# Attention with unscaled exponentials turned, inverse row sums passed through DRAM, and a pair's result divided well behind its softmax

## The chip, the cores and the metric

The kernel runs on one core of a Trainium2 chip as one program. Its time is the device time of one execution in microseconds. Before the change it is 2454.31 us, the median of three runs (2453.69 to 2454.6).

The profile takes one more execution apart, engine by engine. PE is TensorE's matmul side and PEld its weight loads. DVE is VectorE, ACT is ScalarE, POOL is GpSimd, and SP is SyncE, which here does little but issue loads. A name such as L962 is a line of the kernel, numbered as in the version before unless "of after" stands with it. A row of the trace names a tile that is written and the tiles read (`t<-t,rs`), and its shape as partitions x elements.

## What is computed

Two layers of a streaming encoder over 512 tokens of width 1024. A layer is a feed-forward part, a mixer and another feed-forward part. The mixer has three branches: A is attention with a learned bias by distance, B multi-scale pooling, C attention with forget gates. The change concerns A and C alone, with 8 heads of width 64 each.

```python
# branch A (chunked) and branch C (causal), per head
p = softmax(logits + bias, axis=-1)        # over the keys
out = einsum('bhnqk,bnkhd->bnqhd', p, v)
...
branch = einsum('bsnw,nwd->bsnd', stack([ya, yb, yc], axis=2), w_branch)
gates = sigmoid(g_lin.reshape(B, S, 3, D_MODEL))
merged = sum_n(gates * branch)
return merged @ w_out
```

The softmax divides each row of exponentials by its sum. The product with v is linear in the row, so that the division may stand before it or behind it.

## The kernel before

**Numbers in two parts.** Almost every product is made of three matmuls: an operand is kept as a high part (fp32r) and the rest that the rounding leaves (lo). `triple` (L117 to L122) issues hi x hi, hi x lo and lo x hi. `split_to` (L377 to L379) makes such a pair: ACT casts the high part (L378), and DVE, or another engine where one is given, subtracts it from the source (L379).

**The order of work.** The program counts its matmul work in `pe[0]`; one unit is a matmul of 128x512. `later(delay, fn, group)` puts a piece of work on a list, due at `pe[0] + delay`; `poll()` runs what is due, `poll(group="a")` all that belongs to branch A, and `poll(True)` all there is. So a delay such as LAG_T = 24 says how many units of other matmuls are issued between a piece of work and the next that depends on it. A scheduler then decides the order on each engine and which buffer a tile gets; tiles of one tag take turns in a fixed number of buffers (17 of "b", 3 of "t2", 2 of "t1", 2 of "strip", 1 of "ssum"; 4 each of "mm" and "acc" in PSUM).

**Attention** (L940) runs once for A and once for C in each layer: 4 times, 32 heads, 128 query tiles, 16 pairs of heads. For head h and query tile i (128 queries, (i+1)*128 keys):

- `logits`: PE makes the scores with two matmuls (L951, L952; L953 and L954 of after). DVE subtracts them from the bias strip and takes the row's extreme in one instruction (L955). ACT takes the exponential and sums the row (L959). DVE inverts the sum (L961), and the exponentials are multiplied by it in place, on POOL for i < 3 and on DVE for i = 3 (L962).
- `turn`, LAG_T = 24 units later: PE transposes the row blocks (L974), ACT casts the high part out of PSUM (L978), DVE makes the low part (L979). They go to tiles "pta" and "ptb".
- `weigh`, LAG_V = 14 units after every second turn: PE multiplies by v (L996, L997), 256 queries at a time. Both parts of v stand beside each other, so that a head's result comes out in two halves of partitions; ACT copies one (L1000) and DVE adds the other (L1001). `split_to` splits the sum, 64x256, with ACT for the high part and POOL for the low part.

A tile of `ys` holds the two heads of a pair on its 128 partitions, high and low parts of all 512 queries.

Between the query tiles a "filler" issues other matmuls: during A's attention the projections of q, k and v for C and its forget gates; during C's attention the merge of branch A (`merge_units`), which reads `ys`. Ahead of the merge's first product `poll(group="a")` forces everything of A that is still on the list.

POOL's other work in these stretches: a fill of A's bias strips behind their load (L926), masks of C's strips (L937), and in the mixer's later part additions of the merge. SP issues the loads of weights and strips. The copy of x to DRAM is issued from POOL (L1119).

Of the kernel before, what the change touches and what calls it, by code (L numbers as in the profile page):

```python
# [15 lines left out]
F32 = mybir.dt.float32  # L16
F32R = mybir.dt.float32r
I32 = mybir.dt.int32
AF = mybir.ActivationFunctionType
ALU = mybir.AluOpType  # L20
AX = mybir.AxisListType

P = 128
T = 512
# [6 lines left out]
HD = 64  # L31
NT = T // P
# [8 lines left out]
def encoder_kernel(tc, xT, c, w_ada, b_ada, gains, w_gate, w_up, w_down, w_qkv, w_f, w_ubg,  # L41
                   qk_gain, rel, fbias, w_pool, pool_scale, w_branch, w_out, inv_cnt, w_first, out):
    nc = tc.nc
    pools = []

    def open_pool(**kw):
        p = tc.tile_pool(**kw)
        pools.append(p)
        return p.__enter__()
# [4 lines left out]
    dr = open_pool(name="dr", bufs=1, space=bass.MemoryType.DRAM)  # L54
# [3 lines left out]
    NB, NRAW = 17, 2  # L58

    def nm(s):  # L60
        uid[0] += 1
        return f"{s}_{uid[0]}"

    def st(shape, dt, tag, bufs):
        return sb.tile(shape, dt, tag=tag, bufs=bufs, name=nm(tag))
# [4 lines left out]
    def mmt(shape=(P, T)):  # L70
        return ps.tile(list(shape), F32, tag="mm", bufs=4, name=nm("mm"))

    def blk(tag, dt=F32R):
        bufs = {"xv": 4, "v2": 4, "b": NB}[tag]
        return st([P, 2, T], dt, tag, bufs)

    def t1(cols=T):
        return st([P, cols], F32, "t1", 2)

    def t2(cols=T):  # L80
        return st([P, cols], F32, "t2", 3)
# [16 lines left out]
    def later(delay, fn, group=None):  # L98
        t = Task(pe[0] + delay, fn, group)
        tasks.append(t)  # L100
        return t

    def poll(everything=False, group=None):
        if polling[0]:
            return
        polling[0] = True
        while True:
            ready = [t for t in tasks if t.fn is None or everything or t.due <= pe[0]
                     or (group is not None and t.group == group)]
            if not ready:  # L110
                break
            t = min(ready, key=lambda z: z.due)
            tasks.remove(t)
            t.run()
        polling[0] = False
# [56 lines left out]

    x_dram = dr.tile([4, P, 2 * T], F32, name="x_dram")
    fv_dram = [dr.tile([H, FVLEN], F32, name=f"fv_dram{l}") for l in range(L)]

    last = {}

# [199 lines left out]
    def split_to(hi, lo, src, lo_eng=nc.vector):  # L377
        nc.scalar.copy(hi, src)  # L378
        lo_eng.tensor_tensor(lo, src, hi.bitcast(F32), op=ALU.subtract)  # L379
# [502 lines left out]
    def finish_turns(upto=3):  # L882

        for todo in turns:
            while len(todo) >= 4 - upto:
                todo.pop(0)()
# [53 lines left out]
    def attention(qs, ks, vs, strip, ys, filler, budget, group):  # L940


        open_pt = {}

        def logits(h, i, strips):
            p, off = divmod(h, 2)
            (q, ql), k = qs[p], ks[p]
            odd = h % 2
            n = (i + 1) * P
            s = mmt()  # L950
            mm(s[:, :n], q[:, odd, i * P:(i + 1) * P], k[:, odd, :n], start=True, stop=False)  # L951
            mm(s[:, :n], ql[:, odd, i * P:(i + 1) * P], k[:, odd, :n], start=False, stop=True)  # L952
            lg = t1(T)[:, :n]  # L953
            mx = st([P, 1], F32, "mx", 4)  # L954
            nc.vector.tensor_tensor_reduce(out=lg, in0=s[:, :n], in1=strips[i], scale=-1.0, scalar=BIG,  # L955
                                           op0=ALU.add, op1=ALU.min, accum_out=mx)
            pr = t2(T)[:, :n]
            sm = st([P, 1], F32, "sm", 4)
            nc.scalar.activation(pr, lg, AF.Exp, bias=mx, scale=-1.0, accum_out=sm)  # L959
            rs = st([P, 1], F32, "rs", 4)  # L960
            nc.vector.reciprocal(rs, sm)  # L961
            (nc.vector if i == NT - 1 else nc.gpsimd).tensor_scalar(pr, pr, rs, None, op0=ALU.mult)  # L962
            pe[0] += 0.5 * (i + 1.5)
            later(LAG_T, lambda: turn(h, i, pr), group)

        def turn(h, i, pr):
            half, c = divmod(i, 2)
            nj = 2 * half + 2
            if c == 0:
                open_pt[h] = st([P, 2, nj, 256], F32R, "ptb" if half else "pta", 2 if half else 1)  # L970
            pt = open_pt[h]
            tp = mmt()
            for j in range(i + 1):
                nc.tensor.transpose(tp[:, j * P:(j + 1) * P], pr[:, j * P:(j + 1) * P], ident)  # L974
            tv = tp[:, :(i + 1) * P].rearrange("p (j q) -> p j q", q=P)
            dh = pt[:, 0, :i + 1, c * P:(c + 1) * P]
            dl = pt[:, 1, :i + 1, c * P:(c + 1) * P]
            nc.scalar.copy(dh, tv)  # L978
            nc.vector.tensor_tensor(dl, tv, dh.bitcast(F32), op=ALU.subtract)  # L979
            pe[0] += 0.55 * (i + 1)  # L980
            if c == 1:
                later(LAG_V, lambda: weigh(h, half, pt), group)

        def weigh(h, half, pt):
            p, off = divmod(h, 2)
            rows = slice(off * HD, off * HD + HD)
            other = slice(HD - off * HD, 2 * HD - off * HD)
            if off == 0 and half == 0:
                ys.append(blk("b"))
            y = ys[p]  # L990
            o = mmt((P, HALF))
            nj = 2 * half + 2
            for j in range(nj):
                q0 = P if j == nj - 1 else 0
                v2 = vs[j][:, h, :, :].rearrange("p a d -> p (a d)")
                mm(o[:, q0:], v2, pt[:, 0, j, q0:], start=(j == 0), stop=False)  # L996
                mm(o[:, q0:], v2, pt[:, 1, j, q0:], start=False, stop=(j == nj - 1))  # L997
            cols = slice(half * HALF, (half + 1) * HALF)
            yl = t1(T)[:, :HALF]
            nc.scalar.copy(yl[rows, :], o[other, :])  # L1000
            nc.vector.tensor_tensor(yl[rows, :], o[rows, :], yl[rows, :], op=ALU.add)  # L1001
            split_to(y[rows, 0, cols], y[rows, 1, cols], yl[rows, :], nc.gpsimd)
            pe[0] += 1.0 * nj

        for h in range(H):
            strips = strip(h)
            if group == "c":
                finish_turns(h // 2)
            for i in range(NT):
                logits(h, i, strips)  # L1010
                if i == NT - 1:
                    heads[0] = h + 1
                poll()
                goal = pe[0] + budget
                while filler is not None and pe[0] < goal:
                    if next(filler, "end") == "end":
                        filler = None
                poll()
        if filler is not None:
            for _ in filler:  # L1020
                pass

    LAG_T, LAG_V = 24, 14


    def pool_front(l, g):
# [77 lines left out]
    class Mixer:  # L1104
# [10 lines left out]
        def run(self, nxt):  # L1115
# [19 lines left out]

            lo_share[0] = LO_SHARE
            attention(qa, ka, va, lambda h: strip_a(l, h), ya, fill_a(), FILL_A, "a")
            heads[0] = H

# [23 lines left out]
            def fill_c():  # L1163
                yield from merge_units(l, 0, ya, put_a)

            attention(qc, kc, vc, lambda h: strip_c(l, h), yc, fill_c(), FILL_C, "c")
            finish_turns()
            turns.clear()
# [102 lines left out]
```

## Time and profile before

| | |
|---|---|
| runs, median (lowest to highest) | 2454.31 us (2453.69 to 2454.6) |
| profiled execution | 2450.88 us, with a span of 2448.9 us |
| attention stretches | 490 to 700 us and 1695 to 1910 us of the span |

The span begins with the first and ends with the last instruction of the profile. The first view of a profile gives the busy time of each engine; one of the later ones the groups of instructions, each with its line, engine, operation, shape, count, busy us, mean ns, and the idle time of the engine just ahead of them. In the bracket of a row in order of time stands the idle time ahead of that instruction and what ended it. Matmuls overlap: a row's length is longer than the distance of two starts.

### The profile page before, as it was taken

The page shows a single profiled execution, that of the slowest core. Times are in us where ns is not written, and L with a number is a line of the kernel's source. Part 1 is how long each engine was busy: PE and PEld are TensorE (multiplying, and loading weights), DVE is VectorE, ACT ScalarE, POOL GpSimd, SP SyncE. Part 2 cuts the span into 40 slices and gives each one's busy share as a digit, 9 for nine tenths or more (in the row PEclk, how much of TensorE's full clock was granted, in tenths as well). Part 3 has the DMA queues.
Part 4 walks back from the last instruction along what each step waited for, and adds up shares of the span by engine and source line. Part 5 has one row for each costly group of instructions (what it writes and reads, how often), then busy time and mean ns, then how long its engine had stood idle before and what let it go on. Part 6 is the DMA issues. An engine that isn't in the chain of part 4 may idle for free. (4 is left out here: it accounts for less than half of the span.)

```text
span 2448.9 us, 34028 instructions
## 1 busy us (share of the span) xinstructions
PE 2396.8 (98%) x12966; PEld 2051.8 (84%) x12966; DVE 1600.5 (65%) x2859; ACT 1110.3 (45%) x1888; POOL 377.3 (15%) x439
## 2 busy tenths in 40 slices
PE   7999999999999999999999999999999999999999
PEld 5798888777888898988898888878777888988888
DVE  8978766677643378787678656477765434765463
ACT  5333345677642353333453334366765333533341
POOL 3000002144532110000000000123354322000000
PEclk9999999999999999999999999999999999999999
DMA  7756543222323426565327423223133234233232
GB/s 284 251 170 209 198 147 113 78 82 88 116 91 103 142 75 240 174 206 198 129 85 243 138 86 121 103 90 96 61 109 99 95 111 139 87 104 112 67 114 78
DMA packets 116279, 320.23 MB, mean 131 GB/s; under 512 B 11122, under 2 KB 13298, under 8 KB 116116
## 3 DMA queue, kind: packets, MB, share of 16 engines
q1 hardware_dynamic: 114962, 313.86, 38.3%
q0 software_dynamic: 1152, 4.19, 0.4%
q8 instruction: 102, 1.67, 0.3%
q14 instruction: 61, 0.50, 0.1%
q10 hardware_dynamic: 2, 0.00, 0.0%
HBM read 311.64 MB, written 6.38 MB: 130 GB/s over the span
## 5 line engine op out<-in xcount | busy, mean ns | idle before, releaser
L271 ACT CAST whi<-raw 128x1024 fp32r<-128x1024 f32 (+1 forms) x325 | 338.2, 1044 | 595.1 <-PE mm L120 289.2
L273 DVE TENSOR_TENSOR wlo<-raw,whi 128x1024 fp32r<-128x1024 f32 x317 | 392.2, 1240 | 197.4 <-ACT whi L271 194.2
L121 PE MATMUL mm<-hhi,wlo 128*128 128x512 f32 x744 | 289.8, 390 | 0.7 <-DVE wlo L273 0.4
L119 PE MATMUL mm<-hhi,whi 128*128 128x512 f32 x744 | 290.2, 390 | 0.0
L120 PE MATMUL mm<-hlo,whi 128*128 128x512 f32 x744 | 290.0, 390 | 0.0
L119 PE MATMUL acc<-b,whi 128*128 128x512 f32 (+1 forms) x704 | 264.1, 376 | 1.7 <-ACT b L378 1.7
L121 PE MATMUL acc<-b,wlo 128*128 128x512 f32 (+1 forms) x704 | 262.1, 374 | 3.5 <-DVE wlo L273 3.5
L120 PE MATMUL acc<-b,whi 128*128 128x512 f32 (+1 forms) x704 | 262.4, 373 | 0.0
L197 DVE CUSTOM_DVE_ANT_0 v<-v,b,badac 128x1024 f32<-128x1024 f32 x144 | 188.3, 1316 | 60.9 <-DMA v<-in_w_ada_dram 60.7
L119 PE MATMUL acc<-hhi,whi 128*128 128x512 f32 x480 | 190.7, 399 | 1.7 <-ACT hhi L738 1.7
L121 PE MATMUL acc<-hhi,wlo 128*128 128x512 f32 x480 | 188.9, 394 | 0.0
L120 PE MATMUL acc<-hlo,whi 128*128 128x512 f32 x480 | 188.5, 393 | 0.2 <-DVE hlo L741 0.2
L121 PEld LDWEIGHTS mm<-hhi,wlo 128*128 128x128 f32 x744 | 139.7, 188 | 30.9 <-DVE wlo L273 1.6
L119 PEld LDWEIGHTS mm<-hhi,whi 128*128 128x128 f32 x744 | 140.0, 188 | 27.9
L120 PEld LDWEIGHTS mm<-hlo,whi 128*128 128x128 f32 x744 | 139.7, 188 | 27.4
L121 PEld LDWEIGHTS acc<-b,wlo 128*128 128x128 f32 x704 | 133.8, 190 | 27.2 <-DVE wlo L273 4.6
L119 PEld LDWEIGHTS acc<-b,whi 128*128 128x128 f32 x704 | 133.3, 190 | 23.8 <-ACT b L378 2.6
L120 PEld LDWEIGHTS acc<-b,whi 128*128 128x128 f32 x704 | 133.3, 189 | 23.2 <-DVE b L379 0.9
L119 PE MATMUL acc<-whi,hhi 128*128 128x512 f32 x336 | 137.7, 411 | 4.4 <-ACT t L828 3.7
L120 PE MATMUL mm<-b,whi 128*128 128x512 f32 (+1 forms) x384 | 135.8, 354 | 0.0
L119 PE MATMUL mm<-b,whi 128*128 128x512 f32 (+1 forms) x384 | 135.8, 354 | 0.0
L121 PE MATMUL mm<-b,wlo 128*128 128x512 f32 (+1 forms) x384 | 135.6, 354 | 0.0
(300 smaller groups left out, 5598.3 us busy)
## 6 DMA issues: line engine op xcount, KB each, us to landing
v<-in_w_ada_dram SPq DMA_DIRECT2D x144, 512.0 KB, 4.4
raw<-in_w_down_dram SPq DMA_DIRECT2D x88, 512.0 KB, 3.5
raw<-in_w_up_dram SPq DMA_DIRECT2D x82, 512.0 KB, 3.4
b<-in_w_gate_dram SPq DMA_DIRECT2D x76, 512.0 KB, 5.3
raw<-in_w_ubg_dram SPq DMA_DIRECT2D x56, 512.0 KB, 3.3
raw<-in_w_qkv_dram SPq DMA_DIRECT2D x42, 512.0 KB, 3.7
raw<-in_w_branch_dram SPq DMA_DIRECT2D x24, 512.0 KB, 3.6
raw<-in_w_out_dram SPq DMA_DIRECT2D x16, 512.0 KB, 3.3
```

What stands on the lines that cost most here:

```text
L119: mm(o, lh, rh, start=start, stop=False, skip_group_check=onto)
L120: mm(o, lh, rl, start=False, stop=False, skip_group_check=onto)
L121: mm(o, ll, rh, start=False, stop=stop, skip_group_check=onto)
L197: dot = nc.vector.tensor_tensor_reduce(out=raw, in0=raw, in1=silc[0], scale=1.0, scalar=badac[:, l, j, d:d + 1], op0=ALU.mult, op1=ALU.add ...
L271: nc.scalar.copy(hi, raw)
L273: lo_eng.tensor_tensor(lo, raw, hi.bitcast(F32), op=ALU.subtract)
```

## The change

The reciprocals' place and the division's place are moved behind the product with v:

- The exponential's row sums of a head go to one tile [128, 4], a column for each query tile. After the fourth tile one reciprocal inverts all four columns (L965 of after). Nothing scales the exponentials; `turn` transposes them as they are.
- The inverses have queries on partitions; the result of `weigh` has queries along the row. So a DMA issued from POOL writes the [128, 4] tile to a row of DRAM in the order of the queries (L966 of after), 512 numbers of 4 bytes.
- LAG_R = 50 units later `spread` issues a second DMA from POOL: it reads the row and writes it to the 64 partitions of this head (L1011 of after), in the second half of a tile "b" named `rows_of[p]`. `weigh`'s add writes its sum straight to the first half.
- LAG_N = 36 units behind the odd head's spread, `norm_rows` takes a new tile "b", multiplies the pair's sums by the spread inverses on DVE (L1020 of after, 128x512), and splits the product with ACT and DVE (L379 and L380 of after, 128x512).

```diff
+    inv_dram = {(g, p): dr.tile([2, T], F32, name=f"inv_dram_{g}{p}") for g in "ac" for p in range(4)}
...
+        sums, rows_of = {}, {}
...
             pr = t2(T)[:, :n]
-            sm = st([P, 1], F32, "sm", 4)
-            nc.scalar.activation(pr, lg, AF.Exp, bias=mx, scale=-1.0, accum_out=sm)
-            rs = st([P, 1], F32, "rs", 4)
-            nc.vector.reciprocal(rs, sm)
-            (nc.vector if i == NT - 1 else nc.gpsimd).tensor_scalar(pr, pr, rs, None, op0=ALU.mult)
+            if i == 0:
+                sums[h] = st([P, NT], F32, "sm", 3)
+            nc.scalar.activation(pr, lg, AF.Exp, bias=mx, scale=-1.0, accum_out=sums[h][:, i:i + 1])
+            if i == NT - 1:
+                rs = st([P, NT], F32, "rs", 3)
+                nc.vector.reciprocal(rs, sums[h])
+                nc.gpsimd.dma_start(inv_dram[group, p][odd].rearrange("(i q) -> q i", q=P), rs)
+                later(LAG_R, lambda: spread(h), group)
...
             if off == 0 and half == 0:
-                ys.append(blk("b"))
-            y = ys[p]
+                rows_of[p] = st([P, 2, T], F32, "b", NB)
+            y = rows_of[p][:, 0, :]
...
             nc.scalar.copy(yl[rows, :], o[other, :])
-            nc.vector.tensor_tensor(yl[rows, :], o[rows, :], yl[rows, :], op=ALU.add)
-            split_to(y[rows, 0, cols], y[rows, 1, cols], yl[rows, :], nc.gpsimd)
+            nc.vector.tensor_tensor(y[rows, cols], o[rows, :], yl[rows, :], op=ALU.add)
             pe[0] += 1.0 * nj
+
+        def spread(h):
+            p, off = divmod(h, 2)
+            nc.gpsimd.dma_start(rows_of[p][off * HD:(off + 1) * HD, 1, :],
+                                inv_dram[group, p][off:off + 1, :].broadcast_to([HD, T]))
+            if off:
+                later(LAG_N, lambda: norm_rows(p), group)
+
+        def norm_rows(p):
+            y = blk("b")
+            ys.append(y)
+            full = rows_of[p][:, 0, :]
+            nc.vector.tensor_tensor(full, full, rows_of[p][:, 1, :], op=ALU.mult)
+            split_to(y[:, 0, :], y[:, 1, :], full)
...
-    LAG_T, LAG_V = 24, 14
+    LAG_T, LAG_V, LAG_R, LAG_N = 24, 14, 50, 36
```

The three places below show how instructions stand on an engine, in the order of its queue; there is no time in them. A row has the line, the operation, the tiles (their numbers differ between the versions) and the shape.

POOL in the attention of C, early in the first layer's: t is a tile of exponentials, rs an inverse sum, strip and ssum the bias strips, b a pair's result.

```order
L962 TENSOR_SCALAR t_1113_5638<-t_1113_5638,rs_5641 128x256
L962 TENSOR_SCALAR t_1120_5666<-t_1120_5666,rs_5669 128x384
L937 TENSOR_TENSOR strip_5898<-strip_5898,cmask 128x128 x3
L379 TENSOR_TENSOR b_5589<-t_1128_5695,b_5589 64x256
L937 TENSOR_TENSOR ssum_5743<-ssum_5743,cmask 128x128
L962 TENSOR_SCALAR t_1146_5755<-t_1146_5755,rs_5758 128x128
L379 TENSOR_TENSOR b_5589<-t_1150_5769,b_5589 64x256
L962 TENSOR_SCALAR t_1161_5800<-t_1161_5800,rs_5803 128x256
```

The same stretch of after:

```order
L938 TENSOR_TENSOR strip_5760<-strip_5760,cmask 128x128 x3
L966 DMA inv_dram_c_127<-rs_5594 128x4x1
L938 TENSOR_TENSOR ssum_5620<-ssum_5620,cmask 128x128
L1011 DMA b_5477<-inv_dram_c_127 64x512
L938 TENSOR_TENSOR strip_5902<-strip_5902,cmask 128x128 x3
L966 DMA inv_dram_c_128<-rs_5738 128x4x1
L938 TENSOR_TENSOR ssum_5762<-ssum_5762,cmask 128x128
L1011 DMA b_5780<-inv_dram_c_128 64x512
```

POOL has no scaling and no subtraction of results left there; the masks of the next head's strips now alternate with the two DMAs of a head.

DVE in the attention of C, from the end of one head's logits into the next head's: mm is a PSUM tile, pta and ptb the turned exponentials, mx the row's extreme.

```order
L961 RECIPROCAL rs_5956<-sm_5954 128x1
L979 TENSOR_TENSOR ptb_5891<-mm_5962,ptb_5891 128x4x128
L955 ISA t_1210_5978,mx_5979<-mm_5975,strip_5898 128x384
L955 ISA mx_5979 128x1
L979 TENSOR_TENSOR pta_5987<-mm_5988,pta_5987 128x128
L961 RECIPROCAL rs_5984<-sm_5982 128x1
L1001 TENSOR_TENSOR t_1218_6007<-mm_5998,t_1218_6007 64x256
L955 ISA t_1221_6023,mx_6024<-mm_6020,ssum_5900 128x512
```

The same place of after:

```order
L984 TENSOR_TENSOR ptb_5895<-mm_5961,ptb_5895 128x4x128
L957 ISA t_1185_5977,mx_5978<-mm_5974,strip_5902 128x384
L957 ISA mx_5978 128x1
L984 TENSOR_TENSOR pta_5982<-mm_5983,pta_5982 128x128
L1006 TENSOR_TENSOR b_5780<-mm_5993,t_1191_6002 64x256
L1020 TENSOR_TENSOR b_5780<-b_5780 128x512
L984 TENSOR_TENSOR pta_5982<-mm_6008,pta_5982 128x2x128
L957 ISA t_1194_6017,mx_6018<-mm_6014,ssum_5904 128x512
```

The reciprocals between are gone. The product L1020 stands directly behind the add of the odd head's last weighing, ahead of the next low part L984 and the next L957.

PE at the hand-over of A's last pair to the merge: b_5311 (before) and b_5539 (after) are the result of pair 3, whi and wlo weights of the merge, hhi and hlo the layer's input, acc the merge's sums.

```order
L951 MATMUL mm_5632<-b_5107,b_4550 128x256
L952 MATMUL mm_5632<-b_5107,b_4551 128x256
L119 MATMUL acc_5674<-b_5311,whi_5402 128x512
L120 MATMUL acc_5674<-b_5311,whi_5402 128x512
L121 MATMUL acc_5674<-b_5311,wlo_5403 128x512
```

The same place of after:

```order
L119 MATMUL acc_5662<-hhi,whi_5658 128x512
L120 MATMUL acc_5662<-hlo,whi_5658 128x512
L121 MATMUL acc_5662<-hhi,wlo_5659 128x512
L119 MATMUL acc_5553<-b_5539,whi_5299 128x512
L119 MATMUL acc_5604<-b_5539,whi_5299 128x512
L979 MATMUL mm_5612<-ident,t_1067_5549 128x128
L120 MATMUL acc_5553<-b_5539,whi_5299 128x512
```

Before, scores of a head of C stand directly ahead of the first matmul that reads the pair; in after, matmuls of a gate (hhi with whi) are placed ahead of it.

## The prediction, made before the changed kernel ran

> **What bounds the kernel now.** The page's first lines come first: who is busy, and for how long.
>
> ```profile
> span 2448.9 us, 34028 instructions
> PE 2396.8 (98%) x12966; PEld 2051.8 (84%) x12966; DVE 1600.5 (65%) x2859; ACT 1110.3 (45%) x1888; POOL 377.3 (15%) x439
> ```
>
> PE (TensorE's matmuls) is busy 98% of the span, and the change takes away no matmul and adds none. It can only win idle time of PE. POOL's 377.3 us are no limit as such; POOL matters where PE waits for it. So the second view is busy time by stretch (length, then busy us of PE, PEld, DVE, ACT, POOL with their counts), for the first layer's two attentions, for the second layer's, and for a stretch of FFN.
>
> ```profile
> 490.00:700.00 210.00, 198.19 (x1037) 159.37 (x1036) 144.55 (x375) 138.22 (x313) 98.59 (x131) 0.99 0.30 95
> 1695.00:1910.00 215.00, 201.84 (x1055) 161.14 (x1054) 147.50 (x378) 140.45 (x316) 100.42 (x133) 1.00 0.30 91
> 1100.00:1310.00 210.00, 209.18 (x1256) 186.83 (x1255) 149.97 (x262) 90.26 (x145) 9.32 (x9) 1.00 0.43 145
> ```
>
> PE stands idle for 210 - 198.19 = 11.8 us and 215 - 201.84 = 13.2 us in the attentions, 25.0 us together, and for 0.8 us in the FFN stretch. These 25 us, 1.0% of the span, are all that can be won. The third view says who ends that idle time: PE's waits (matmul line and releaser, total us, times, longest). Lines from L940 to L1001 are attention's.
>
> ```profile
> PE mm L974 <- POOL t L962: 6.8, 15, 0.7
> PE mm L951 <- DVE t L1001: 4.6, 6, 1.1
> PE mm L951 <- DVE ptb L979: 3.0, 2, 1.5
> PE mm L951 <- DVE b L859: 1.8, 2, 0.9
> PE mm L951 <- DVE mx L955: 1.8, 4, 0.7
> PE mm L974 <- DVE ptb L979: 1.7, 4, 0.5
> PE mm L974 <- DVE rs L961: 1.0, 2, 0.5
> ```
>
> The first row is the wait that the change is about: the transposes L974 wait for POOL's scaling of the exponentials. With the last row (reciprocal) that is 7.8 us in 17 waits. The other five make 12.9 us in 18 waits: logits L951 or transposes behind DVE work that came late.
>
> One such wait in order of time (start, length; the bracket is the drawn idle time):
>
> ```profile
> 513.77 0.39 PE L120 MATMUL acc<-wlo,hhi 128*128 128x512 f32 x1
> 514.00 0.40 PE L121 MATMUL acc<-whi,hlo 128*128 128x512 f32 x1
> 514.08 0.93 POOL L962 TENSOR_SCALAR t<-t,rs 128x256 f32<-128x256 f32 x1 [5.50 <-DVE rs L961]
> 515.06 0.33 PE L974 MATMUL mm<-ident,t 128*128 128x128 f32 x1 [0.66 <-POOL t L962]
> ```
>
> Matmuls follow each other every 514.00 - 513.77 = 0.23 us (my unit below), though each is drawn 0.40 long. The transpose could have started at 514.23 and started at 515.06: 0.83 us lost, 0.66 drawn. A drawn wait hides about 0.17 us more.
>
> **The change part by part.** Two layers have 4 attentions, 32 heads, 128 query tiles and 16 pairs of heads. Rows of groups: line, engine, shape and count, then busy us, mean ns, idle before.
>
> ```profile
> L961 DVE RECIPROCAL rs<-sm 128x1 f32<-128x1 f32 x128 | 20.2, 159 | 37.7 <-ACT t L959 37.6
> L962 DVE TENSOR_SCALAR t<-t,rs 128x512 f32<-128x512 f32 x32 | 16.6, 520 | 1.2
> L962 POOL TENSOR_SCALAR t<-t,rs 128x384 f32<-128x384 f32 x32 | 39.9, 1248 | 37.2 <-DVE rs L961 26.8 <-PE mm L974 5.7 <-PE acc L121 2.4
> L962 POOL TENSOR_SCALAR t<-t,rs 128x256 f32<-128x256 f32 x32 | 29.6, 926 | 33.0 <-DVE rs L961 23.0 <-DVE nt_q L285 3.7 <-PE acc L121 3.3
> L962 POOL TENSOR_SCALAR t<-t,rs 128x128 f32<-128x128 f32 x32 | 19.4, 606 | 68.1 <-DVE rs L961 67.9
> L378 ACT CAST b<-t 64x256 fp32r<-64x256 f32 x64 | 25.9, 404 | 26.7 <-DVE t L1001 26.3
> L378 ACT CAST b<-b 128x512 fp32r<-128x512 f32 x14 | 8.2, 622 | 0.7 <-DVE b L499 0.7
> L379 POOL TENSOR_TENSOR b<-t,b 64x256 fp32r<-64x256 f32 x64 | 56.4, 882 | 94.5 <-ACT b L378 93.4
> L379 DVE TENSOR_TENSOR b<-b,b 128x512 fp32r<-128x512 f32 x14 | 9.1, 681 | 0.0
> L839 DVE TENSOR_TENSOR ptb<-ptb,nt_z 128x512 f32<-128x512 f32 x16 | 18.8, 1216 | 0.2
> L1119 POOL DMA_DIRECT2D x_dram<-xv x8 | 4.8, 603 | 647.7 <-DVE xv L430 647.3
> ```
>
> *A, the scaling goes.* A transpose then waits for the exponential itself. The longest drawn wait, 0.7 us, is about the shortest POOL scaling (0.606 us) with the reciprocal before it (0.159 us), so what is late next, the exponential, should be there in nearly all 17 places. Gain: 7.8 + 17 x 0.17 = **10.7 us**.
>
> *B, less traffic ahead of the other waits.* DVE loses 96 of 128 reciprocals (15.3 us) and 32 scalings (16.6), and gains 16 multiplications and 16 subtractions of 128x512. No such product stands in the trace; the nearest rows are 681 ns and, beside a busy POOL, 1216 ns. I take 681, since POOL has less to do then: +21.8, net -10.1 us (-1.5 at 1216). ACT loses 64 casts that stood at the head of its queue for 26.3 us behind L1001's add, and gains 16 x 622 ns = 10.0: net -16 us of work. POOL loses 145.3 us and gains 64 DMA issues, by L1119 603 ns each (38.6 us). So DVE's and ACT's chains come earlier, by tenths of a microsecond. The 12.9 us in 18 waits are worth 12.9 + 18 x 0.17 = 16.0; nothing to all of it may go. I take a fifth, **3.2 us**, since 10 of DVE's 292 us in the attention stretches is only 3%, and most of these waits hang on the order of the queue, which stays.
>
> *C, the new waits.* The row of inverses goes out (L966 of after) and comes back to 64 partitions (L1011), 64 small DMAs in all. Their flight is not in the trace. The nearest rows (bytes each, us from issue to landing):
>
> ```profile
> out_dram<-xv SPq DMA_DIRECT2D x8, 128.0 KB, 1.7
> x_dram<-xv POOLq DMA_DIRECT2D x8, 512.0 KB, 3.2
> b<-in_w_qkv_dram SPq DMA_DIRECT2D x6, 512.0 KB, 6.9
> ```
>
> Store and read after each other take between 2 x 1.7 = 3.4 us and 2 x 6.9 = 13.8 us; I take 5.5, nearer to the small one, with a POOL issue and reciprocal between. What needs the row is DVE's product L1020, which stands right behind the add of the odd head's second weighing (L1001 before, L1006 after). How long after the reciprocal does that add run? In group a's last head, in c's fourth and in c's last:
>
> ```profile
> 585.03 0.16 DVE L961 RECIPROCAL rs<-sm 128x1 f32<-128x1 f32 x1 [0.21 <-ACT t L959]
> 597.56 0.41 DVE L1001 TENSOR_TENSOR t<-mm,t 64x256 f32<-64x256 f32 x1
> 628.38 0.15 DVE L961 RECIPROCAL rs<-sm 128x1 f32<-128x1 f32 x1
> 636.76 0.43 DVE L1001 TENSOR_TENSOR t<-mm,t 64x256 f32<-64x256 f32 x1 [0.22 <-ACT t L1000]
> 679.04 0.15 DVE L961 RECIPROCAL rs<-sm 128x1 f32<-128x1 f32 x1
> 685.15 0.43 DVE L1001 TENSOR_TENSOR t<-mm,t 64x256 f32<-64x256 f32 x1 [1.86 <-ACT t L1000]
> 689.10 1.23 DVE L273 TENSOR_TENSOR wlo<-raw,whi 128x1024 fp32r<-128x1024 f32 x1 [0.26 <-ACT whi L271]
> ```
>
> To the end of the add that is 597.97 - 585.03 = 12.9 us, 637.19 - 628.38 = 8.8 and 685.58 - 679.04 = 6.5. A flight of 5.5 us is over by then, so the product does not wait. Where that cover fails, the price is rival 1's. What remains is small: pair 3 of group a, which the merge reads at once, now goes through product, cast and subtraction (0.681 + 0.622 + 0.681 = 2.0 us) after its last add where before a cast and a POOL subtraction (0.404 + 0.882 = 1.3) did: 0.7 us later, twice. Some masks and fills of POOL stand behind a DMA that waits at its queue's head; L951 can wait for them through the next strip. Together **-2 us**, between 0 and -6 (a wait of 1.5 us, the longest in the list above, at each of the 4 attentions).
>
> The sum: 10.7 + 3.2 - 2 = 11.9 us. From the profiled execution, 2450.88 us (span 2448.9 and 2.0 around it), that leaves 2439.0. The runs shown have a median of 2454.31, 0.14% more, so the forecast there is **2442 us**. With the ends of B and C it lies between 10.7 - 6 = 4.7 and 10.7 + 16.0 = 26.7 us of gain, 2450 to 2428.
>
> **The rivals.**
>
> *1, slower: the round trip outlasts its cover.* Then DVE stands at L1020 with everything behind it: the lo halves L979, the fused L955, the weights' L273. PE has some slack before that reaches it: a weighing is due 14 units (3.2 us) behind its turn, of which cast and subtraction take 0.622 + 0.681 = 1.3 us at the most (the rows above), so 2 us. In group c three pairs a layer have a cover of 8.8 + 2 = 10.8 us, 6 places; its last pair has 6.5 us and DVE's pause to 689.10, some 10 + 2 = 12 us, 2 places; group a's 12.9 + 2 is never reached. At 13.8 us the price is 6 x 3.0 + 2 x 1.8 = 21.6, and the time 2454.3 - 11.9 + 21.6 = **2464 us**. It outweighs the gain from 6(T - 10.8) + 2(T - 12) = 11.9, T = 12.6 us. For it: the store takes its words one by one, 4 bytes from each of 128 partitions to addresses in four rows, and nothing in the trace is like it; against it: 2 KB in all, and 12.6 us is seven times the row of 1.7. [...]
>
> *2, no change: the gain is given back.* The scheduler also moves transposes forward, by up to three matmuls (0.7 us) in a few places, and the exponential has a queue of its own on ACT: a transpose that waited 0.45 us (6.8 / 15) for POOL may wait as long for ACT. If A gives only a third (3.6) and B nothing, 3.6 - 2 leaves **2452 us**. For it: A is 17 small waits among 128 query tiles, each soon taken up by another lateness; against it: the reciprocal and POOL's 0.6 to 1.2 us are taken out of every chain, and nothing is put in.
>
> *3, more: the queues were what held PE.* If two thirds of B go (10.7), A + B - C = 19.4, and the time is **2434 us**. For it: ACT's 26.3 us at the head of its queue; against it: DVE still issues the lo halves in the same order.
>
> **How the numbers follow.** The forecast gets 0.53, rival 2 0.20, rival 3 0.12, rival 1 0.15. A measurement of this kernel can tell about 0.2%, 4.9 us: the forecast and rival 3 are faster (0.65), rival 2 is the same (0.20), rival 1 slower (0.15). The range reaches below from rival 3 by 3 us for the end of B (2431) and above past rival 2 to 2457, a round trip just over its break-even; outside stay most of rival 1 and a little below 2431.
>
> **What would show it.** A is right if the profile of the changed kernel has no wait of the transposes for POOL, and their waits for the exponential total under 2 us; B, if L951's waits for DVE fall from 11.2 us by a few; C, if DVE's wait of the product for its DMA is near nothing, and the spread lands under 8 us behind its reciprocal. PE's idle time in both attentions should fall from 25 us to about 13. Long waits of DVE at the product with PE waits behind them mean rival 1; a row of the transposes waiting for ACT with the same total as POOL's now means rival 2. The forecast would also be wrong if PE's own busy time changed, say because a moved transpose breaks the pace of 0.23 us.

## The result, and the profile after

The changed kernel takes 2556.74 us (median of 4 runs, 2554.39 to 2559.22) beside 2454.0 us for the kernel before, measured with it: a ratio of 1.0421, with a 95% interval from 1.0403 to 1.0439. It is 4.2% slower. The forecast was 2442 us, with a range up to 2457; the slower side had a chance of 0.15, with 2464 us as its price.

The page's first lines and the first layer's attention stretch (length, busy us of PE, PEld, DVE, ACT and POOL, mean granted clock of PE, DMA share, GB/s) of the changed kernel:

```profile
span 2552.5 us, 33716 instructions
PE 2419.1 (95%) x12966; PEld 2073.9 (81%) x12966; DVE 1587.4 (62%) x2763; ACT 1092.8 (43%) x1840; POOL 267.7 (10%) x343
490.00:700.00 210.00, 169.96 (x870) 138.88 (x868) 117.41 (x289) 112.07 (x255) 39.70 (x71) 0.91 0.39 85
```

As the change says, POOL, DVE and ACT all do less than before. PE, with the same 12966 matmuls, stands idle for 40 us of this stretch where it was 11.8. It is also busy 22 us longer in all, at a granted clock of 0.91 in the stretch, which was 0.99. PE's longest new waits, and then DVE's (line, releaser, total us, times, longest):

```profile
PE mm L979 <- DVE mx L957: 30.1, 4, 11.4
PE mm L1001 <- DVE pta L984: 25.2, 4, 6.9
PE mm L979 <- ACT t L962: 18.8, 4, 9.4
DVE b L1020 <- DMA b<-inv_dram_c: 81.9, 8, 13.4
DVE b L1020 <- DMA b<-inv_dram_a: 37.3, 7, 10.0
DVE t L957 <- POOL strip L938: 13.0, 2, 7.8
```

The wait of the transposes for POOL is gone. In its place DVE stands for 119 us at the product L1020 until the spread row has come, and PE waits for what is queued behind the product. The last row is a second, smaller way to the same loss: POOL's queue stands at the spread until the store has landed, the masks L938 behind it come late, and L957 waits for them. It happens once in each layer, for 7.8 us (there the strip itself was 3.4 us later still) and 5.2 us, and two of the four PE waits in the first row follow from it (6.8 and 4.2 us). The DMA rows (bytes each, median us from issue to landing) show where the time goes:

```profile
strip<-fv_dram SPq DMA_DIRECT2D x16, 384.0 KB, 11.1
b<-inv_dram_c POOLq DMA_DIRECT2D x16, 128.0 KB, 5.2
inv_dram_a<-rs POOLq DMA_DIRECT2D x16, 2.0 KB, 10.0
inv_dram_c<-rs POOLq DMA_DIRECT2D x16, 2.0 KB, 10.4
```

One of the smallest transfers, 2 KB of inverses, is among the slowest: 10 us. And a bystander has become slow too: the strips of C's attention need 11.1 us now. Before, their row was

```profile
strip<-fv_dram SPq DMA_DIRECT2D x16, 384.0 KB, 3.6
```

One round trip late in C's attention, in order of time, from the timelines of DVE, POOL and PE:

```profile
686.94 0.17 DVE L965 RECIPROCAL rs<-sm 128x4 f32<-128x4 f32 x1
690.32 1.64 POOL L938 TENSOR_TENSOR strip<-strip,cmask 128x128 f32<-128x128 f32 x3 [4.09 <-DMA strip<-fv_dram]
691.91 0.79 POOL L966 DMA_DIRECT2D inv_dram_c<-rs  x1
695.35 0.43 DVE L1006 TENSOR_TENSOR b<-mm,t 64x256 f32<-64x256 f32 x1 [2.06 <-ACT t L1005]
701.09 0.53 POOL L1011 DMA_DIRECT2D b<-inv_dram_c  x1 [7.89 <-DMA inv_dram_c<-rs]
704.36 0.69 DVE L1020 TENSOR_TENSOR b<-b 128x512 f32<-128x512 f32 x1 [8.57 <-DMA b<-inv_dram_c]
705.08 0.42 DVE L984 TENSOR_TENSOR pta<-mm,pta 128x256 fp32r<-128x256 f32 x1
705.55 0.58 PE L1001 MATMUL mm<-pta,v 128*128 128x256 f32 x1 [5.96 <-DVE pta L984]
```

From the reciprocal to the product are 704.36 - 686.94 = 17.4 us: 5.0 until POOL issues the store, since the masks ahead of it wait for a strip that is late; 9.2 until the store has landed; 3.3 for the spread. The add L1006 was done at 695.8, so DVE waited 8.6 us, the low part L984 with it, and PE 6.0 us for that. This trip is an ordinary one: over the 16 pairs the product starts 13.7 to 20.7 us after the odd head's reciprocal. The pause has an after-effect, in PE's rows and in windows around it:

```profile
707.00 0.63 PE L120 MATMUL acc<-b,whi 128*128 128x512 f32 x1
707.43 0.63 PE L121 MATMUL acc<-b,wlo 128*128 128x512 f32 x1
705.30:709.00 3.70, 3.44 (x11) 2.92 (x12) 3.14 (x10) 2.83 (x8) 0.79 (x1) 0.54 0.37 89
709.00:713.00 4.00, 4.00 (x23) 3.39 (x22) 2.72 (x9) 1.58 (x5) 1.01 (x1) 1.00 0.32 115
```

Over the 3.7 us around the pause's end and behind it the mean granted clock is 0.54, and matmuls start every 0.43 us instead of 0.23: another 3.7 x 0.46 = 1.7 us for this wait. The clock granted from 705.55 to 708.69 us is 0.50. It had fallen within the pause: the mean over the pause itself (699.59 to 705.55) is 0.69, which puts the fall some 2.3 us into it, an estimate from that mean. A pause of 3.0 us (738.19 to 741.17) was also followed by 0.50, from 742.83 to 746.24 us.

### The profile page after: what moved, and what is told of

It is laid out like the page before. It is cut to its first block, busy times and chain, and to the rows that moved or that the text cites. A ratio compares the mean times of both kernels' runs of the same rounds, so it can differ in the third digit from the quotient of the medians.

```text
span 2552.5 us, 33716 instructions
## 1 busy us (share of the span) xinstructions
PE 2419.1 (95%) x12966; PEld 2073.9 (81%) x12966; DVE 1587.4 (62%) x2763; ACT 1092.8 (43%) x1840; POOL 267.7 (10%) x343
## 5 line engine op out<-in xcount | busy, mean ns | idle before, releaser
L119 PE MATMUL acc<-hhi,whi 128*128 128x512 f32 x480 | 196.4, 410 | 8.9 <-ACT whi L272 7.2
```

What stands on the lines that cost most here:

```text
L119: mm(o, lh, rh, start=start, stop=False, skip_group_check=onto)
```

## The experiments

The theory after this reading, S: the store of 512 words costs the time, in two ways: what waits for it, and what its transfer stops elsewhere. Rivals: O, that the rest of the change is at fault; W, that DVE parked at the product is the whole cost; G, that any small DMA from POOL is slow.

**The trip taken apart.** Each is an edit of the changed kernel.

```diff
# e1_no_trip: no store, and a fill in place of the spread
-                nc.gpsimd.dma_start(inv_dram[group, p][odd].rearrange("(i q) -> q i", q=P), rs)
-            nc.gpsimd.dma_start(rows_of[p][...], inv_dram[...].broadcast_to([HD, T]))
+            nc.gpsimd.memset(rows_of[p][off * HD:(off + 1) * HD, 1, :], 1.0)
# e2_store_only: the store stays, the fill replaces the spread
# e3_spread_only: no store; the spread reads w_down[0, 0, 0:1, :T]
# e4_runs_of_16: the store's order
-                nc.gpsimd.dma_start(inv_dram[group, p][odd].rearrange("(i q) -> q i", q=P), rs)
+                nc.gpsimd.dma_start(inv_dram[group, p][odd].rearrange("(q i) -> q i", q=P), rs)
```

> Leaves out the store of the inverses and the spread; POOL fills the 64x512 rows with 1.0 instead, so that the results are not divided. Theory S (the store of 512 single words is what costs; the rest of the change does what was forecast): 2442 us, between 2434 and 2450, PE idle in the two attention stretches about 13 us. Rival O (the unscaled exponentials, the moved transposes and the later division are themselves at fault): above 2480 us.

> Keeps the store of the inverses, leaves out the spread (a POOL fill with 1.0 in its place), so that nothing waits for the store; the results are not divided. If the loss is only DVE parked at its product for the round trip (theory W): about 2442 us, strip loads as before (3.6 us). Theory S (the store's single words hold the DMA engines, so that other loads behind it stop): strip loads stay near 11 us, and the time stays well above, 2470 to 2530 us.

> Leaves out the store; the spread reads 512 contiguous words of a weight in DRAM instead, so that the results are multiplied by the wrong numbers. Theory S: the spread lands in 2 to 4 us, no long wait of DVE at the product, time within 6 us of e1_no_trip. Rival G (any small DMA issued from POOL is slow here): spread still 5 to 6 us and more, time 2470 us or more.

> The store writes each partition's four inverses beside each other: 128 runs of 16 bytes instead of 512 of 4, the same 2 KB; the row's numbers are in another order, so that results are divided by the wrong sums. Theory S with a cost for each word written: the store's flight falls from 10.2 us to about 2.5 + 7.7/4 = 4.4 us, strip loads below 6 us, and the time to 2440 to 2460 us. If the flight goes by the DMA and not by its runs (rival G): flight near 10 us and time near 2555 us.

Measured beside 2450.8 us for the kernel before: 2427.4 us without the trip (ratio 0.9906, 0.9889 to 0.9922), 2468.6 with the store alone, 2426.4 with the spread alone, 2429.5 with runs of 16 bytes. On that scale the change stands at 1.0421 x 2450.8 = 2554 us. So the rest of the change gains 23 us, more than S expected (2434 to 2450); O falls. The spread costs nothing; G falls. The store costs 2554 - 2427 = 127 us, of which 41 remain when nothing waits for it (2468.6, just below S's 2470), so that W falls as the whole cause. In e2_store_only the strips were late all the same, and so was the last query tile's strip (ssum), which took 3.1 us without the trip:

```profile
strip<-fv_dram SPq DMA_DIRECT2D x16, 384.0 KB, 9.4
ssum<-fv_dram SPq DMA_DIRECT2D x16, 256.0 KB, 9.0
inv_dram_c<-rs POOLq DMA_DIRECT2D x16, 2.0 KB, 10.9
```

With runs of 16 bytes, the same 2 KB, the store lands sooner than the 4.4 us that a price for each run would give, and the time lies below the 2440 that was expected:

```profile
strip<-fv_dram SPq DMA_DIRECT2D x16, 384.0 KB, 3.8
inv_dram_a<-rs POOLq DMA_DIRECT2D x16, 2.0 KB, 2.0
inv_dram_c<-rs POOLq DMA_DIRECT2D x16, 2.0 KB, 3.4
```

**The store by itself.** Two programs of small transfers only. Their core, with DRAM tiles of their own:

```diff
+ nc.gpsimd.dma_start(d.rearrange("o (i q) -> q (o i)", q=P), src)          # words, step of 4 bytes
+ nc.gpsimd.dma_start(d[:, 0:1].rearrange("(i q) o -> q (i o)", q=P), src)  # d is [512, k]: step of 4k bytes
```

> Computes none of the layers: it writes zeros to the output and makes small transfers one after the other, each behind the read-back of the one before, four of each kind. 512 words of 4 bytes as in the change, issued from POOL (words_pool) and from SP (words_sp); 128 words (quarter), 1024 words (double), 512 words each 64 bytes from the next (spaced), 128 runs of 16 bytes (runs), 4 rows of 512 bytes (rows), and 512 words read instead of written (readwords). Theory Word (a price for every single write on its DMA engine): about 10 us for words from either queue and for spaced, 4 for quarter, 18 for double, 2 to 3.4 for runs, 2 for rows. Theory Line (writes of neighbouring words into the same piece of DRAM wait for each other): spaced falls to 4 us or less, the rest as above. Theory Q (the POOL queue is the slow part): words_sp 3 us or less. If reads are as slow, readwords takes 8 us or more.

> Computes none of the layers, as m1_stores. 512 words of 4 bytes to DRAM with a step of 4 bytes (step_a, as in the change), 8 (step_b), 16 (step_c), 32 (step_d), 64 (step_e) and 512 bytes (step_f), and with each partition's four words in its own 128 bytes (own_words); 128 words side by side, one from each partition (one_part); 128 pairs of words (two_words). Then a load of 512 KB issued from SP some 2 us behind a store of step 4 (loadword) and behind one of step 512 bytes (loadstep). Theory Line: step_a 9.2 us, falling with the step to 2.2 at 64 bytes; where it falls is the size of the piece in which words wait for each other; own_words 3 us or less. Theory Hold (the store keeps its DMA engines from all that is behind it): the load behind words lands in 8 us or more, the load behind the wide store in 4 us or less; if it does not hold them, both alike.

DMA rows of m1_stores (a d stands ahead of the name of what is written):

```profile
dwords_pool<-swords_pool POOLq DMA_DIRECT2D x4, 2.0 KB, 9.2
dwords_sp<-swords_sp SPq DMA_DIRECT2D x4, 2.0 KB, 8.9
druns_pool<-sruns_pool POOLq DMA_DIRECT2D x4, 2.0 KB, 1.7
dquarter_pool<-squarter_pool POOLq DMA_DIRECT2D x4, 0.5 KB, 7.5
dspaced_pool<-sspaced_pool POOLq DMA_DIRECT2D x4, 2.0 KB, 2.2
ddouble_pool<-sdouble_pool POOLq DMA_DIRECT2D x4, 4.0 KB, 9.2
readwords_pool<-in_w_down_dram POOLq DMA_DIRECT2D x4, 2.0 KB, 2.5
```

And of m2_steps, with DVE's waits for the load that was issued behind a store:

```profile
dstep_a<-sstep_a POOLq DMA_DIRECT2D x4, 2.0 KB, 8.5
dstep_b<-sstep_b POOLq DMA_DIRECT2D x4, 2.0 KB, 3.7
dstep_c<-sstep_c POOLq DMA_DIRECT2D x4, 2.0 KB, 2.2
dtwo_words<-stwo_words POOLq DMA_DIRECT2D x4, 1.0 KB, 3.3
DVE chain L90 <- DMA vloadword<-in_w_down_dram: 56.0, 4, 14.4
DVE chain L90 <- DMA vloadstep<-in_w_down_dram: 22.1, 4, 5.6
```

It is not the queue: 9.2 us from POOL, 8.9 from SP. It is not the number of words: 128, 512 and 1024 take 7.5, 9.2 and 9.2 us. It is single words that lie side by side in DRAM, each beside words of other partitions: at a step of 8 bytes 512 words take 3.7 us, from 16 bytes on 2.2 us, as long as every wider step tried. Reading 512 single words took 2.5 us. Of the three theories only Line fits the steps, with 16 bytes where 64 were supposed. In size it missed: it gave 4 us for 128 words and 18 for 1024, so that the words wait for each other one by one is not shown.

Hold is seen in its effect: a load behind such a store made DVE wait 56.0 / 4 = 14.0 us, behind a wide one 22.1 / 4 = 5.5. The way is another than the theory's. One store of step_a, issued at 22.47 us, keeps the DMA engines busy for its first 1.7 us (a share of 0.11 up to 24.20) and not at all from there until it lands at 30.92 (0.00). The wide store step_f has the same share in its first 1.7 us. It is the load's own transfers that last: behind the words the engines are busy for 0.99 of the time from 257.70 to 267.60 us at 43 GB/s, behind the wide store for 0.81 from 315.90 to 317.85 at 269 GB/s. Why, no run shows.

The wide store in the kernel, e2_store_only with a step of 16 bytes:

```diff
-    inv_dram = {(g, p): dr.tile([2, T], F32, ...
+    inv_dram = {(g, p): dr.tile([2, T, 4], F32, ...
-                nc.gpsimd.dma_start(inv_dram[group, p][odd].rearrange("(i q) -> q i", q=P), rs)
+                nc.gpsimd.dma_start(inv_dram[group, p][odd][:, 0:1].rearrange("(i q) o -> q (i o)", q=P), rs)
```

> As e2_store_only (nothing waits for the store, results not divided), but the 512 words go to DRAM with a step of 16 bytes instead of 4: as many single words, none beside another. Theory Line (only words side by side are slow): strip loads land in 3 to 4 us, and the time is that of e1_no_trip, 2425 to 2431 us. If single words as such hold the DMA engines: 2460 us or more, as e2_store_only.

2425.8 us: as many single words, 43 us less than e2_store_only, nothing left of the store's cost.

**The product later.** Two ways to give the trip more time in the changed kernel.

```diff
# f2_later_product
-    LAG_T, LAG_V, LAG_R, LAG_N = 24, 14, 50, 36
+    LAG_T, LAG_V, LAG_R, LAG_N = 24, 14, 50, 90
# g1_pinned_product: LAG_N = 60, and
+            last["turn"] = nc.vector.tensor_tensor(dl, tv, ...).ins
+            with after("turn"):
                 nc.vector.tensor_tensor(full, full, rows_of[p][:, 1, :], op=ALU.mult)
```

> The change with the product 54 units (12 us) later, LAG_N 90 instead of 36. Theory W (only DVE parked at the product costs): back to 2430 to 2440 us. Theory S (the store also holds other loads): DVE's waits at the product shrink from 119 us to under 30, strip loads stay near 11 us, and the time is near that of e2_store_only, 2460 to 2490 us.

> The change with the product pinned behind the last turn's low part that was issued before it, and LAG_N 60, so that DVE's queue holds it later by one to two query tiles of the next head. Theory W (only DVE parked at the product costs): 2430 to 2445 us. Theory S (both costs): DVE's waits at the product fall well below 119 us, and the time lies between e2_store_only and the change, 2465 to 2510 us.

f2_later_product took 2543.3 us (ratio 1.0379), and DVE still waited 81.6 + 32.9 = 114.5 us at its product. It did not test what it was made for: the scheduler decides the order of DVE's queue, and in 14 of 16 places the product kept its neighbours although its lag was longer. With the pin it moved: 2496.3 us (1.0183), and

```profile
DVE b L1021 <- DMA b<-inv_dram_c: 38.7, 6, 13.3
strip<-fv_dram SPq DMA_DIRECT2D x16, 384.0 KB, 10.0
```

DVE waited 38.7 us for C's rows and 12.4 for A's instead of 119 in all, with strips as late as ever. That is between e2_store_only and the change, as theory S has it.

**Where the gain comes from.** Three edits of the kernel before.

```diff
# p1_no_scaling
-            rs = st([P, 1], F32, "rs", 4)
-            nc.vector.reciprocal(rs, sm)
-            (nc.vector if i == NT - 1 else nc.gpsimd).tensor_scalar(pr, pr, rs, None, op0=ALU.mult)
# p2_pair_split: scaling stays; sums go to one tile a pair, split at 128x512
-            nc.vector.tensor_tensor(yl[rows, :], o[rows, :], yl[rows, :], op=ALU.add)
-            split_to(y[rows, 0, cols], y[rows, 1, cols], yl[rows, :], nc.gpsimd)
+            nc.vector.tensor_tensor(y[rows, cols], o[rows, :], yl[rows, :], op=ALU.add)
...
+            split_to(y[:, 0, :], y[:, 1, :], rows_of[p])
# h1_low_on_dve
-            split_to(y[rows, 0, cols], y[rows, 1, cols], yl[rows, :], nc.gpsimd)
+            split_to(y[rows, 0, cols], y[rows, 1, cols], yl[rows, :], nc.vector)
```

> The kernel before without the reciprocal and the scaling, so that results are not divided; weighing and splitting as before. This is step A with its share of B: 10.7 us gained by step A alone, 2440 us; if the scaling's removal carries all of the 23 us that e1_no_trip gained, 2428 us; if the gain is all in the weighing's split, 2450 us.

> The kernel before with its scaling, but weighing writes its sums to one tile for the pair, which ACT and DVE split 128x512 at a time at the place where the change does; the whole computation is done. This is the second half of the change alone. p1_no_scaling gained 18 us and e1_no_trip 23, so if the halves add up, 5 us: 2445 us. If the longer way from the last weighing to the result costs: 2450 or more.

> The kernel before with one word changed: weighing's low part (64x256) is made on DVE instead of POOL; scaling stays. Theory P (POOL's queue was the shared limit: its subtraction waits there for ACT's cast, and the scaling of the next exponentials stands behind it): the waits of the transposes for POOL shrink from 15 to 5 or fewer and the time comes near that of p2_pair_split, 2433 to 2440 us. Theory A (the scaling's own length is what PE waits for): 15 waits stay, 2448 to 2455 us.

p1_no_scaling took 2432.2 us (0.9926, 0.9913 to 0.994), p2_pair_split 2433.2 (0.9927, 0.9912 to 0.9941), h1_low_on_dve 2440.7 (0.9961, 0.9947 to 0.9975). Either half of the change gains 18 us and both together 23, not 36: for the most part they relieve the same thing. PE's waits for POOL's scaling in p2_pair_split, and in h1_low_on_dve:

```profile
PE mm L977 <- POOL t L963: 1.7, 5, 0.4
PE mm L974 <- POOL t L962: 6.8, 10, 1.9
```

With the split gone from POOL and made pairwise, the scaling, as long as before, is hardly waited for. With only the subtraction moved to DVE, 9 us are gained, but the transposes wait for POOL as long in total as before (6.8 us). So POOL's queue alone is not the answer, and neither theory gave what was measured. What gives the other 8 us of p2_pair_split was not taken apart: it may be ACT's cast, which no longer stands behind the add, or DVE's load, 1604.4 us there and 1621.5 in h1_low_on_dve.

**A version that beats both.** e4_runs_of_16 with DVE's product reading the row in the order in which it was stored; and the same with the pin.

```diff
# f1_runs_permuted: e4_runs_of_16, and
+            inv = rows_of[p][:, 1, :].rearrange("r (q i) -> r i q", q=P)
+            nc.vector.tensor_tensor(full.rearrange("r (i q) -> r i q", q=P), full.rearrange("r (i q) -> r i q", q=P),
+                                    inv, op=ALU.mult)
# g2_runs_pinned: the same inside
+            with after("turn"):
```

> As e4_runs_of_16, with DVE's product reading the spread row in the order in which it was stored (a step of 16 bytes), so that the whole computation is done. Theory S: 2429 us, between 2425 and 2435, ratio about 0.991. If DVE pays for the step (up to twice the 0.69 us of a product, 16 products): at most 11 us more, 2440.

> f1_runs_permuted with the same pin and LAG_N 36. If the 13.7 us that DVE still waits at the product there matter: 2427 to 2430 us, as e1_no_trip. If they are covered: 2432, no difference to f1_runs_permuted beyond 2 us.

f1_runs_permuted took 2431.8 us (0.9923, 0.991 to 0.9937), g2_runs_pinned 2427.3 (0.9902, 0.9885 to 0.9918), as fast as with no trip at all. DVE's waits at the product for C's rows are 13.7 us in 6 places in the first and 7.4 in 2 in the second. With two words of the store's access pattern swapped and the product reading in the same order, the change is 0.8% faster than the kernel before instead of 4.2% slower, and 1.0% with the product pinned as well. Reading at a step of 16 bytes makes DVE's product longer, 1095 ns in f1_runs_permuted beside 696 in the change, 6.4 us over 16 products.

## Why the prediction was wrong, point by point

**What bounds the kernel** was read rightly: PE, and its waits in the attentions. The loss came there too, with a second part that the prediction had no term for. Against g2_runs_pinned (span 2426.6, PE busy 2389.2) the change has 133.4 - 37.4 = 96 us more idle time of PE and 30 us more busy time with the same matmuls. Of the 30 us, 28 are the slower clock in and behind the long pauses: at half clock PE was busy 69 us in the change and 13 in g2_runs_pinned, and half of the difference is lost.

**A and B**, 10.7 + 3.2 = 13.9 us, were right in kind and too small: 23.4 us without the trip, nearly the 26.7 that all of A and B were said to be worth at most. Which of the two was mis-sized the runs do not separate: if A was right, B was worth 12.7 us and not 3.2, but A's own edit (p1) gained 18.2, and the other half, with the scaling left in place (p2), 17.6. The halves show that the waits listed under different releasers were not separate sums. Of A's 7.8 us nothing is left in p1 and 3.4 in p2; of the five other rows' 12.9 us, 8.7 are left in p1 and 6.8 in p2. Either half shortened both lists.

The waits are also not the whole gain, and here the prediction was wrong: it said that the change can only win idle time of PE. The span of e1_no_trip is 23.1 us shorter than that of before; 14.5 us of it are idle time of PE (52.1 to 37.6 us), and 8.6 are busy time with the same matmuls (2396.8 to 2388.2). The prediction's 0.17 us for each of 35 waits hides 6.0 us at the most in the busy time; what else is in it stays open.

With no trip the transposes' wait for POOL was gone, and hardly a wait for the exponential took its place; in h2_wide_store_only PE's row for it is

```profile
PE mm L979 <- ACT t L962: 0.2, 1, 0.2
```

So rival 2 is refuted as a mechanism. Rival 3 came nearer for this half, 2427 us beside its 2434; that two thirds of B went is not shown, since A and B cannot be told apart. (By their own sums rival 2's time is 2452.7 and rival 3's 2434.9 us.)

**C** is the step that failed: "Store and read after each other take between 2 x 1.7 = 3.4 us and 2 x 6.9 = 13.8 us; I take 5.5, nearer to the small one", and with it "so the product does not wait". By the medians of the changed kernel store and spread took 10.4 + 5.2 = 15.6 us in C and 10.0 + 6.0 = 16.0 in A, nearly three times the 5.5 and beyond the upper end. In the trip shown they took 9.2 + 3.3 = 12.5 us, and the other 5.0 of its 17.4 passed before POOL issued the store. For a store that stands behind masks the prediction had no term; for masks behind a DMA it had 1.5 us at each attention, where 7.8 and 5.2 were measured at two. Both ends came from rows of 128 KB and 512 KB transfers, and the value was put near the smaller; the time of this store hangs on how its words lie (8.5 us at a step of 4 bytes, 2.2 at 16, m2_steps). The prediction named that the words go one by one and that nothing in the trace is like it, and still judged its time by its size. For a store in runs of 16 bytes the 5.5 would have been about right: 2.0 + 3.2 = 5.2 us in A and 3.4 + 3.5 = 6.9 in C (e4_runs_of_16).

**Rival 1** is what happened, in its mechanism, its place and its side; its size was far off. It priced 2464 us, 10 more than before, and 103 more were measured. Three things were not in its price. The trip of 17.4 us puts its formula at 6 x 6.6 + 2 x 5.4 = 50 us instead of 21.6, where 127 - 41 = 86 came with the waiting. It let A's attention off, since the cover of 12.9 us there was taken as out of reach; DVE waited 37.3 us there. And it left out what the store does to others, 41 us with nobody waiting for it, and the clock. Issuing from POOL is not the cause: from SP the store took 8.9 us, from POOL 9.2 (m1_stores).

## What to carry to other kernels

Before a small transfer is put between two engines, look at how its words lie in DRAM, not at its bytes: here single words of different partitions side by side took 9.2 us where the same 2 KB in runs of 16 bytes took 1.7 (m1_stores), and strip loads of 3.6 us took 9.4 with such stores about (e2_store_only); the reader could undo the order for 0.4 us of DVE a product. A wait that parks an engine costs what is queued behind it: here DVE's wait of 8.6 us kept PE idle for 6.0, and after that pause matmuls started every 0.43 us instead of 0.23. A delay written in the program moves a waiting instruction only where the scheduler follows it; look for it in the engine's queue.

## What the runs showed of the hardware

- In the programs of small transfers (m1_stores, m2_steps) a store of 512 words of 4 bytes from 128 partitions took 8.5 to 9.2 us at a step of 4 bytes in DRAM (8.9 from SP), 3.7 at 8 and 2.2 at 16 to 512, while 128 words side by side took 7.5. Why neighbours are slow, and in pieces of what size, no run shows; reading 512 such words took 2.5 us.
- With such stores about, loads issued from SP were late: strip loads of 3.6 us took 9.3 (f2_later_product) to 11.1 (the change), and in m2_steps DVE waited 8.5 us longer for the load than behind a wide store. The store itself kept the DMA engines busy for its first 1.7 us only (a share of 0.11, m2_steps).
- After a pause of 6.0 us PE was granted 0.50 of its clock for 3.1 us, and full speed afterwards; over an attention stretch with several such pauses the mean was 0.91 (both in the change).
